# A pad of 32 bytes ahead of the right-hand tiles, and the sums of the down weights moved from the retention stage to the gate/up stage

## The chip, the cores and the metric

The kernel runs on one core of a Trainium2 chip. The metric is device time in microseconds (us). Before the change it is 1449.94 us, the median of 3 runs (1449.83 to 1451.63 us). TensorE is called PE in the rows (its weight loads PEld), VectorE DVE, ScalarE ACT, GpSimd POOL, and SyncE, which issues all DMAs here, SP.

## The reference

One decoder layer for 1024 tokens of 1024 features, in float32:

```python
xn = rmsnorm(h, pre_mix_norm)
mix = token_mixer(xn, ...)            # retention (4 heads) beside latent attention (8 heads), then w_o
h = h + rmsnorm(mix, post_mix_norm)
hn = rmsnorm(h, pre_ffn_norm)
ff = (silu(hn @ w_gate) * (hn @ w_up)) @ w_down      # inner width 2816
h = h + rmsnorm(ff, post_ffn_norm)
e = rmsnorm(p @ w_ple_proj, ple_norm)
h = h + e * sigmoid(h @ w_ple_gate + b_ple_gate)
```

## The kernel before, in words

Every large matmul is done in three products of float32r parts: an operand is split into a high part (a cast on ACT) and a low part (a subtraction, mostly on DVE), and PE adds high by high, high by low and low by high (`split` and `products`, L79 to L95).

The stages follow one another: the input projection, the latent projections, retention (L404 to L547), latent attention (L548 to L675), the output projection with its norms (L686 to L751), gate/up (L756 to L862), down (L864 to L953) and the last gate (`pg`, L955 to L979).

The three matrices of the feed-forward part are multiplied by a Strassen scheme: seven products of half blocks in place of eight, with sums of blocks as operands. The inner width is cut into 11 groups `q`. In gate/up each group has a gate and an up matrix (`m`), each with seven products of 12 matmuls of 128 by 512: 14 steps and 168 matmuls per group, 154 steps and 1848 matmuls in all. Per matrix, SP loads 1 MB (`load`), POOL makes the sums (`weight_sums`, four operations of 128x512), and ACT and DVE split (`weight_part`). Per group POOL makes the sums of the activations (`down_operands`, four operations), which SP stores to `ld`.

Down reads `ld`, `w_down` and `td`: the four sums of blocks of the down weights, t1 = b12 - b11, t2 = b22 - t1, t3 = b22 - b12, t4 = b21 - t2, stored in DRAM. They depend on nothing but the input. Before the change `down_sums(q)` (L408) makes them during retention: two loads of 512 KB into the pool `raws`, four POOL operations of 128x512 (`combos`, L107) into a third `raws` tile and over the loaded ones, three stores (512, 256 and 256 KB). `raws` has four buffers, and the retention weights go through the same four.

The tile framework plans the order of the instructions on each engine when the program is built: work goes ahead of its place in the code where its tiles are free. On the chip each engine and each DMA queue then takes its instructions in that order, and a waiting one holds up those behind it.

Tiles lie in an SBUF partition from the left or from the right (`side="right"`). In the built program the right end is byte 229344, which is 3583 * 64 + 32, and all sizes on that side are multiples of 64, so every right-hand tile starts 32 bytes past a multiple of 64: `bh1` and `bl1` (196576 and 212960), the gate/up weights `graw`, `gh`, `gl` (`gh` from 180192), and the down and last weights `draw`, `dh`, `dl` (`dh` from 135136). The large left-hand tiles start at multiples of 64: `bh0` (19136), `hi` and `lo` of the ring, `xh` and `xl` (19136, 76480), `mh`, `ml`, `h2h`, `h2l`. So the two operands of a matmul are either in step (their distance is a multiple of 64 bytes) or 32 bytes out of step.

In the profile a matmul's names stand as out<-moving,stationary. Of the wide matmuls, these are out of step before the change: all of gate/up (`gu`: moving `xh`, stationary `gh`), all of `pg` (moving `dh_pg`, stationary `h2h`), the output projection `po` at L94 (moving `bh1`), and the second twelve of each 24 in `pqk`, `prg` and `pge` (moving `bh1`, where the first twelve have `bh0`). In step: down (`da`, `db`: both operands on the right) and those first twelve.

Of the kernel before, what the change touches and what calls it, by code (L numbers as in the profile page):

```python
# [11 lines left out]
F32 = mybir.dt.float32  # L12
# [4 lines left out]
ALU = mybir.AluOpType  # L17
# [3 lines left out]
P = 128  # L21
S = 1024
# [11 lines left out]
NQ = NF // 2  # L34
# [28 lines left out]
def hybrid_layer(ctx: ExitStack, tc: tile.TileContext, a: dict, out: bass.AP):  # L63
    nc = tc.nc
    act, dve, pool, pe, sp = nc.scalar, nc.vector, nc.gpsimd, nc.tensor, nc.sync
# [3 lines left out]
    dram = ctx.enter_context(tc.tile_pool(name="dram", bufs=1, space=DRAM))  # L69
# [6 lines left out]
    def ps1(name, tag="t"):  # L76
        return (ps if tag == "t" else psf).tile([P, 512], F32, tag=tag, name=name)
# [29 lines left out]
    def combos(t1, t2, t3, t4, b11, b12, b21, b22, eng):  # L107
        eng.tensor_tensor(out=t1, in0=b12, in1=b11, op=ALU.subtract)
        eng.tensor_tensor(out=t2, in0=b22, in1=t1, op=ALU.subtract)
        eng.tensor_tensor(out=t3, in0=b22, in1=b12, op=ALU.subtract)  # L110
        eng.tensor_tensor(out=t4, in0=b21, in1=t2, op=ALU.subtract)

    def scoped(stack, name, bufs=1, **kw):
        return stack.enter_context(tc.tile_pool(name=name, bufs=bufs, reuse_waits="tile", **kw))
# [6 lines left out]
    def bcast(stack_pool, src, name):  # L121
        t = stack_pool.tile([P, D], F32, name=name, bufs=1)
        sp.dma_start(out=t, in_=src.broadcast_to([P, D]))
        return t

    pack = const.tile([P, sum(PACK.values())], F32, name="pack")
    mhalf = const.tile([P, 32], F32, name="mhalf")
    pool.memset(mhalf, -0.5)
# [16 lines left out]
    od = [dram.tile([P, D], F32, name=f"od{t}") for t in range(NT)]  # L145
    mo = [dram.tile([P, 4, P], F32, name=f"mo{t}") for t in range(NT)]
    ld = [dram.tile([7, P, 512], F32, name=f"ld{q}") for q in range(NQ)]
    td = [dram.tile([4, P, 512], F32, name=f"td{q}") for q in range(NQ)]


    st1 = ExitStack()
# [8 lines left out]
    raws = scoped(st1, "raws", 4)  # L160
# [67 lines left out]
    for t in range(NT):  # L228
# [36 lines left out]
        out=angm,  # L265
        in0=posf.unsqueeze(2).broadcast_to([P, NT, HR]),
        in1=inv.unsqueeze(1).broadcast_to([P, NT, HR]),
        op=ALU.mult,
# [19 lines left out]
    for hf in range(2):  # L288
        for b in (3, 4, 0, 1, 2):
# [3 lines left out]
            w = wq[:, b : b + 1] if b < 3 else wkv[:, b - 3 : b - 2]  # L293
            cs = slice(hf * 512, (hf + 1) * 512)
# [21 lines left out]
    for j in range(NH // 2):  # L316
        pt = ps2(f"pk{j}")
        for hf in range(2):
            cs = slice(hf * 512, (hf + 1) * 512)
# [26 lines left out]
    for j in range(NH // 2):  # L346
        pt = ps2(f"pq{j}")
        for hf in range(2):
            cs = slice(hf * 512, (hf + 1) * 512)
# [45 lines left out]
    for i in range(2):  # L395
        hs, cs = slice(i * RA, (i + 1) * RA), slice(i * H2, (i + 1) * H2)
# [7 lines left out]
    pr = scoped(stk, "pr", 2)  # L404
    tri = pr.tile([P, P], F32, name="tri", bufs=1)
    sp.dma_start(out=tri, in_=a["tri"])

    def down_sums(q):  # L408
        r1, r2, s = [raws.tile([P, S], F32, tag="raw", name=n) for n in ("wd1", "wd2", "wds")]
        sp.dma_start(out=r1, in_=a["w_down"][q][:, 0:2, :].rearrange("p i n -> p (i n)"))  # L410
        sp.dma_start(out=r2, in_=a["w_down"][q][:, 2:4, :].rearrange("p i n -> p (i n)"))
        c0, c1 = slice(0, 512), slice(512, S)
        combos(s[:, c0], s[:, c1], r1[:, c1], r2[:, c0], r1[:, c0], r1[:, c1], r2[:, c0], r2[:, c1], pool)
        sp.dma_start(out=td[q][0:2].rearrange("i p n -> p i n"), in_=s.rearrange("p (i n) -> p i n", i=2))
        sp.dma_start(out=td[q][2], in_=r1[:, c1])
        sp.dma_start(out=td[q][3], in_=r2[:, c0])

    down_q = 0
    g_ret = [1.0 - 2.0 ** (-5.0 - h) for h in range(RH)]
    pending = None  # L420
    for j in range(RH // 2):
# [14 lines left out]
        for hh in range(2):  # L436
            h = 2 * j + hh
# [8 lines left out]
            for hf in range(2):  # L446
                cs = slice(hf * 512, (hf + 1) * 512)
# [28 lines left out]
                for c in range(4):  # L476
                    c1 = slice(c * P, (c + 1) * P)
# [3 lines left out]
                                         in1=tri.unsqueeze(1).broadcast_to([P, 4, P]), op0=ALU.mult, op1=ALU.mult)  # L481
                pkt = ps1("pkt")
                for c in range(4):
                    c1 = slice(c * P, (c + 1) * P)
# [4 lines left out]
                for c in range(4):  # L489
                    c1 = slice(c * P, (c + 1) * P)  # L490
                    pe.matmul(pu[:, c1], kz[:, c1], vt[:, hf * 4 + c, hh * RD : (hh + 1) * RD], start=True, stop=True)
                rs = [rprev]
                for c in range(4):
                    if hf == 1 and c == 3:
                        break
                    c1 = slice(c * P, (c + 1) * P)
# [3 lines left out]
                    else:  # L500
                        dve.scalar_tensor_tensor(out=rn, in0=rs[-1], scalar=_f32(np.exp(np.float32(P) * np.log(np.float32(g_ret[h])))),
                                                 in1=pu[:, c1], op0=ALU.mult, op1=ALU.add)
# [36 lines left out]
                if pending is not None:  # L539
                    pending()  # L540
                pending = finish
                for _ in range(1 + (hf and h > 0)):
                    if down_q < NQ:
                        down_sums(down_q)
                        down_q += 1
        pending()
        pending = None  # L547
    va = pv.tile([P, NT, 2 * VD], F32R, tag="va", name="va")  # L548
# [47 lines left out]
    for h in range(NH):  # L596
        kh_, kl_, qh, ql = heads(h) if h else first
        if h == 2:
            for k in range(RH):
                raw = raws.tile([P, S], F32, tag="raw", name=f"mr{k}")  # L600
                sp.dma_start(out=raw, in_=md[k])
                for c in range(2):
                    cs = slice(c * 512, (c + 1) * 512)
# [8 lines left out]
        for gg in range(2):  # L612
            cs = slice(gg * 512, (gg + 1) * 512)
            po = ps1("po", "of"[gg] if h >= 3 else "o")
            for g in (2 * gg, 2 * gg + 1):
                pb = []
                sc = ps2("sc") if g < 2 else None
                for i in (2 * g, 2 * g + 1):
                    n = (i + 1) * P
                    c1 = slice(i * P, (i + 1) * P)  # L620
# [4 lines left out]
                    w = max(n // nc_, 256)  # L625
                    for c in range(nc_):
                        products(sc[:, o + c * 512 : o + c * 512 + w],
                                 [(qh[:, c1], ql[:, c1], kh_[:, c * w : (c + 1) * w], kl_[:, c * w : (c + 1) * w])])
                    w = n // nc_
# [3 lines left out]
                        out=sv, in0=sv, in1=cmask[:, S - n :].rearrange("p (c n) -> p c n", c=nc_),  # L633
# [122 lines left out]
    st_g = ExitStack()  # L756
# [2 lines left out]
    gs = scoped(st_g, "gs", 3)  # L759
    gev = scoped(st_g, "gev", 1)  # L760
    gga = scoped(st_g, "gga", 2)

    mats = [(name, q) for q in range(NQ) for name in ("w_gate", "w_up")]
    raw, sums, parts, bank, part_sums, act_out = {}, {}, {}, {}, {}, {}
# [26 lines left out]
    def use(m, b, v):  # L791
        name, q = mats[m]
        dst = act_out[q][:, KEPT[b]]
        if name == "w_gate":
            act.activation(dst, v, AF.Silu)
        else:
            dve.tensor_tensor(out=dst, in0=v, in1=dst, op=ALU.mult)  # L797

    def product(m, n):
# [24 lines left out]
        else:  # L824
            nm, blk = {1: ("s1", 0), 4: ("s5", 3), 5: ("u2", 1)}[n]
            dve.tensor_tensor(out=s[nm], in0=dst, in1=s[nm], op=ALU.add)  # L826
            use(m, blk, s[nm])

    def down_operands(q):
        ga = act_out[q]  # L830
        s = gs.tile([P, 3, HALF], F32, tag="s", name="dsums")
        pool.tensor_tensor(out=s[:, 1], in0=ga[:, 2], in1=ga[:, 3], op=ALU.add)  # L832
        pool.tensor_tensor(out=s[:, 0], in0=s[:, 1], in1=ga[:, 0], op=ALU.subtract)
        pool.tensor_tensor(out=s[:, 2], in0=ga[:, 1], in1=s[:, 0], op=ALU.subtract)
        pool.tensor_tensor(out=ga[:, 2], in0=ga[:, 0], in1=ga[:, 2], op=ALU.subtract)
        sp.dma_start(out=ld[q][0:4].rearrange("i p n -> p i n"), in_=ga)
        sp.dma_start(out=ld[q][4:7].rearrange("i p n -> p i n"), in_=s)
# [16 lines left out]
    for i, (m, n) in enumerate(steps):  # L854
        for _, f, args in sorted(todo[i], key=lambda x: x[0]):
            f(*args)
        product(m, n)
        if m % 2 == 0 and m and n == 1:
            down_operands(m // 2 - 1)
    down_operands(NQ - 1)  # L860
    st_g.close()
    st_x.close()  # L862
# [9 lines left out]
    def dslot(srcs, name, sub=dve):  # L872
        n = len(srcs)
        raw = draw.tile([P, D], F32, tag="raw", name=f"raw_{name}")
        for i, src in enumerate(srcs):
            sp.dma_start(out=raw[:, i * (D // n) : (i + 1) * (D // n)] if n > 1 else raw[:, : src.shape[-1]], in_=src)
        m = sum(src.shape[-1] for src in srcs)
        hi, lo = [dring.tile([P, D], F32R, tag=h, name=f"{h}_{name}")[:, :m] for h in ("dh", "dl")]
        split(hi, lo, raw[:, :m], sub=sub)
        return hi, lo  # L880
# [2 lines left out]
        return lambda q: a["w_down"][q][:, i, :]  # L883

    def td_quad(i):
        return lambda q: td[q][i]

    bank_b = [ps1("db", n) for n in "ttfo"]
    bank_a2 = [ps2("da") for _ in range(2)]
    bank_a = [bank_a2[j // 2][:, (j % 2) * HALF : (j % 2 + 1) * HALF] for j in range(4)]  # L890

    def down(li, rhs, banks, fresh):
        for c in range(0, NQ, 2):
            qs = range(c, min(c + 2, NQ))
            lh, ll = dslot([ld[q][li] for q in qs], "l")
            rh, rl = dslot([rhs(q) for q in qs], "r")
            for n, q in enumerate(qs):
                for j in range(4):
                    ls = slice(n * HALF + j * P, n * HALF + (j + 1) * P)
                    rs_ = slice(n * HALF, (n + 1) * HALF)  # L900
                    for m, (l, r) in enumerate(((lh, rh), (lh, rl), (ll, rh))):
                        pe.matmul(banks[j], l[:, ls], r[:, rs_], start=(fresh and q == 0 and m == 0),  # L902
                                  stop=(q == NQ - 1 and m == 2), skip_group_check=True)
# [19 lines left out]
    wpo = bcast(ph, a["w_postf"], "wpo")  # L923
    wpl = bcast(ph, a["w_plen"], "wpl")
    bg = bcast(ph, a["b_pg"], "bg")
    down(4, td_quad(1), bank_b, False)
    for j in range(4):
        act.copy(out=acc[2 * j][:, d2], in_=bank_b[j])
    down(5, td_quad(0), bank_a, True)
    for j in range(4):  # L930
        act.copy(out=acc[2 * j + 1][:, d2], in_=bank_a[j])
    down(6, wd_quad(3), bank_a, False)
    for j in range(4):
        dve.tensor_tensor(out=acc[2 * j][:, d2], in0=bank_a[j], in1=acc[2 * j][:, d2], op=ALU.add)
    down(2, td_quad(2), bank_b, False)
    for j in range(4):
        dve.tensor_tensor(out=acc[2 * j + 1][:, d2], in0=bank_b[j], in1=acc[2 * j + 1][:, d2], op=ALU.add)
    for j in range(4):
# [8 lines left out]

    for j in range(4):
        features(2 * j)
    down(3, td_quad(3), bank_b, False)  # L950
    for j in range(4):
        act.copy(out=acc[2 * j + 1][:, d1], in_=bank_b[j])

# [4 lines left out]
    for n, t in enumerate([0, 2, 4, 6, 1, 3, 5, 7]):  # L958
# [10 lines left out]
        for c in range(2):  # L969
            cs = slice(c * 512, (c + 1) * 512)  # L970
            products(pt[:, cs], [(gh[k // 4][:, k % 4, ts], gl[k // 4][:, k % 4, ts], wg[k][0][:, cs], wg[k][1][:, cs]) for k in range(8)])
        z = draw.tile([P, D], F32, tag="raw", name="z")
        for c in range(2):
            cs = slice(c * 512, (c + 1) * 512)
# [76 lines left out]
```

## Time and profile before

| | |
|---|---|
| median of 3 runs | 1449.94 us |
| the profiled execution | 1453.09 us, of which the span from first to last instruction is 1451.3 us |
| PE busy | 1361.4 us, 94% of the span |
| DVE, ACT, POOL busy | 767.4, 538.5 and 427.2 us |
| mean granted clock of PE | 0.976 of 2.4 GHz |

Busy time of PE counts a matmul from start to modelled end, and matmuls overlap, so how fast they follow one another is read from start to start, or from a run of them in the chain of waits divided by their count.

### The profile page before, as it was taken

To read this page: it belongs to the slowest core of one execution; us is meant where nothing else is said; L and a number is where in the kernel's file an instruction comes from. 1 tells how busy PE (TensorE), PEld (TensorE's weight loads), DVE (VectorE), ACT (ScalarE), POOL (GpSimd) and SP (SyncE) were. 2 spreads that over 40 slices of the span, in tenths; PEclk is the share of its full clock that TensorE was granted. 3 is DMA by queue.
4 is the path that set the end of the run, shared out by engine and by line. 5 is a ranking of instruction groups with operands and counts; after the bars stand their busy time and mean duration, and the time that the engine had idled before them with its cause. 6 is when DMAs were issued, how large, how long until landed. Compare 5 with 4: busy or idle time off the path is not lost.

```text
span 1451.3 us, 18194 instructions
## 1 busy us (share of the span) xinstructions
PE 1361.4 (94%) x6732; PEld 1134.0 (78%) x6732; DVE 767.4 (53%) x1198; ACT 538.5 (37%) x889; POOL 427.2 (29%) x333
## 2 busy tenths in 40 slices
PE   7999999999989998876899999999997999999998
PEld 6987988788768886655688888888885788888776
DVE  6456447526577675586344444434443554474653
ACT  5343221111565554344233333333332544444421
POOL 1100344400354243237144444444443000013300
PEclk9999999999999999986999999999999999999999
DMA  6137776812565641661123332232312966575422
GB/s 242 44 123 247 264 266 232 284 52 59 163 202 145 177 113 45 226 236 50 38 109 110 109 109 92 98 109 87 109 58 98 330 203 204 187 239 181 132 72 73
DMA packets 91320, 214.73 MB, mean 148 GB/s; under 512 B 9504, under 2 KB 24096, under 8 KB 88416
## 3 DMA queue, kind: packets, MB, share of 16 engines
q1 hardware_dynamic: 91232, 213.58, 44.2%
q8 instruction: 53, 0.87, 0.3%
q14 instruction: 35, 0.29, 0.1%
HBM read 144.86 MB, written 67.63 MB: 146 GB/s over the span
## 4 chain that ended last, share of the span: by engine, by line
PE 70%; DMA 8%; DVE 7%; issue 5%; POOL 5%; ACT 3%; SPq 1%; DVEq 0%; POOLq 0%; ACTq 0%
PE gu L813 30%; PE da L902 6%; PE pg L94 5%; PE fill L94 4%; PE pa L94 4%; PE db L902 3%; PE sc L94 3%; DMA wd<-in_w_down 2%; PE prg L94 2%; PE ptp L650 2%; PE prv L94 2%; PE pge L94 2%; PE pqk L94 1%; PE po L94 1%; DMA td<-wd 1%
## 5 line engine op out<-in xcount | busy, mean ns | idle before, releaser
L813 PE MATMUL gu<-xh,gh_w_gate 128*128 128x512 f32 x308 | 123.0, 399 | 5.1 <-ACT gh_w_gate L81 1.6
L813 PE MATMUL gu<-xh,gh_w_up 128*128 128x512 f32 x308 | 122.4, 398 | 2.3 <-DVE s L826 0.9
L813 PE MATMUL gu<-xh,gl_w_up 128*128 128x512 f32 x308 | 121.9, 396 | 1.6 <-DVE gl_w_up L82 1.6
L813 PE MATMUL gu<-xl,gh_w_gate 128*128 128x512 f32 x308 | 122.5, 398 | 0.0
L813 PE MATMUL gu<-xh,gl_w_gate 128*128 128x512 f32 x308 | 122.3, 397 | 0.0
L813 PE MATMUL gu<-xl,gh_w_up 128*128 128x512 f32 x308 | 122.0, 396 | 0.0
L119 POOL TENSOR_TENSOR s<-s,mhalf 128x1 f32<-128x1 f32 x32 | 28.6, 901 | 310.3 <-DVE s L117 310.2
L641 POOL TENSOR_TENSOR pr<-pr,ri 128x128 f32<-128x128 f32 (+3 forms) x64 | 73.8, 1164 | 109.3 <-DVE ri L640 97.3
L82 DVE TENSOR_TENSOR dl_r<-raw_r,dh_r 128x1024 fp32r<-128x1024 f32 (+1 forms) x42 | 47.7, 1135 | 81.9 <-ACT dh_r L81 70.4
L832 POOL TENSOR_TENSOR dsums<-ga 128x512 f32<-128x512 f32 x11 | 14.2, 1289 | 250.4 <-DVE ga L797 250.4
L826 DVE TENSOR_TENSOR s<-gu,s 128x512 f32<-128x512 f32 x44 | 30.4, 691 | 102.0 <-PE gu L813 102.0
L81 ACT CAST dh_r<-raw_r 128x1024 fp32r<-128x1024 f32 (+1 forms) x42 | 41.3, 982 | 105.9 <-PE da L902 52.4
L902 PE MATMUL db<-dh_r,dh_l 128*128 128x512 f32 x176 | 68.1, 397 | 8.3 <-ACT dh_r L81 8.3
L813 PEld LDWEIGHTS gu<-xh,gh_w_gate 128*128 128x128 f32 x308 | 58.3, 189 | 20.6 <-ACT gh_w_gate L81 2.0
L813 PEld LDWEIGHTS gu<-xh,gh_w_up 128*128 128x128 f32 x308 | 57.9, 188 | 17.8 <-DVE s L826 1.3
L813 PEld LDWEIGHTS gu<-xh,gl_w_up 128*128 128x128 f32 x308 | 57.9, 188 | 16.0 <-DVE gl_w_up L82 2.1
L902 PE MATMUL db<-dl_r,dh_l 128*128 128x512 f32 x176 | 69.3, 394 | 0.1
L813 PEld LDWEIGHTS gu<-xh,gl_w_gate 128*128 128x128 f32 x308 | 58.2, 189 | 14.3 <-DVE gl_w_gate L82 0.2
L902 PE MATMUL db<-dh_r,dl_l 128*128 128x512 f32 x176 | 69.3, 394 | 0.0
L813 PEld LDWEIGHTS gu<-xl,gh_w_gate 128*128 128x128 f32 x308 | 58.3, 189 | 14.0
L813 PEld LDWEIGHTS gu<-xl,gh_w_up 128*128 128x128 f32 x308 | 58.0, 188 | 13.9
L82 DVE TENSOR_TENSOR tl<-ptp,th 128x512 fp32r<-128x512 f32 (+1 forms) x80 | 49.7, 633 | 24.0 <-ACT th L81 22.8
(337 smaller groups left out, 3807.2 us busy)
## 6 DMA issues: line engine op xcount, KB each, us to landing
raw_l<-ld SPq DMA_DIRECT2D x77, 256.0 KB, 3.3
wd<-in_w_down SPq DMA_DIRECT2D x22, 512.0 KB, 4.7
raw_w_gate<-in_w_gate SPq DMA_DIRECT2D x11, 1024.0 KB, 4.8
raw_w_up<-in_w_up SPq DMA_DIRECT2D x11, 1024.0 KB, 4.8
ld<-ga SPq DMA_DIRECT2D x11, 1024.0 KB, 4.3
raw_r<-td SPq DMA_DIRECT2D x44, 256.0 KB, 4.0
ld<-dsums SPq DMA_DIRECT2D x11, 768.0 KB, 3.6
raw_r<-in_w_down SPq DMA_DIRECT2D x33, 256.0 KB, 4.6
```

The lines of the kernel that those rows point to most:

```text
L81: act.copy(out=hi, in_=src)
L82: sub.tensor_tensor(out=lo, in0=src, in1=hi.bitcast(F32), op=ALU.subtract)
L94: pe.matmul(dst, l, r, start=(m == 0), stop=(m == n - 1))
L119: pool.tensor_tensor(out=dst, in0=dst, in1=mhalf[:, :n], op=ALU.pow)
L641: pool.tensor_tensor(out=pr_[:, :n], in0=pr_[:, :n], in1=ri.broadcast_to([P, n]), op=ALU.mult)
L650: pe.transpose(pt[:, m * P : (m + 1) * P], pb[qq][:, kk * P : (kk + 1) * P], ident)
L813: pe.matmul(dst, l[:, at, ks], r[:, i, k, :], start=(n in (0, 1, 3) and x == 0), stop=(x == 11), skip_group_check=True)
L826: dve.tensor_tensor(out=s[nm], in0=dst, in1=s[nm], op=ALU.add)
L832: pool.tensor_tensor(out=s[:, 1], in0=ga[:, 2], in1=ga[:, 3], op=ALU.add)
L902: pe.matmul(banks[j], l[:, ls], r[:, rs_], start=(fresh and q == 0 and m == 0), stop=(q == NQ - 1 and m == 2), skip_group_check=True)
```

## The change

A pool `pad` with one tile of 8 floats (32 bytes) is opened first on the right, so each right-hand tile starts 32 bytes lower: `bh1` at 196544, `gh` from 180160, `dh` from 135104. Nothing reads or writes the tile.

`down_sums` leaves retention. In gate/up, after steps 2, 5, 8 and 11 of the 14 of each group, `down_sums(q, c)` treats a quarter of the columns: one load of 256 KB (four pieces of 512 bytes per partition) into a tile of the new left-hand pool `gd` with one buffer, four POOL operations of 128x128 that write over the loaded blocks, one store of 256 KB. That is 44 loads, 176 POOL operations and 44 stores. `td` is laid out as [P, 4, 512] instead of [4, P, 512], its blocks in the order T1, T3, T4, T2, and down picks them by these names. The same sums are computed.

```diff
+    pad = ctx.enter_context(tc.tile_pool(name="pad", bufs=1, side="right"))
+    pad.tile([P, 8], F32, name="pad")
...
-    td = [dram.tile([4, P, 512], F32, name=f"td{q}") for q in range(NQ)]
+    td = [dram.tile([P, 4, 512], F32, name=f"td{q}") for q in range(NQ)]
...
-    def down_sums(q):
-        r1, r2, s = [raws.tile([P, S], F32, tag="raw", name=n) for n in ("wd1", "wd2", "wds")]
-        sp.dma_start(out=r1, in_=a["w_down"][q][:, 0:2, :].rearrange("p i n -> p (i n)"))
-        sp.dma_start(out=r2, in_=a["w_down"][q][:, 2:4, :].rearrange("p i n -> p (i n)"))
-        c0, c1 = slice(0, 512), slice(512, S)
-        combos(s[:, c0], s[:, c1], r1[:, c1], r2[:, c0], r1[:, c0], r1[:, c1], r2[:, c0], r2[:, c1], pool)
-        sp.dma_start(out=td[q][0:2].rearrange("i p n -> p i n"), in_=s.rearrange("p (i n) -> p i n", i=2))
-        sp.dma_start(out=td[q][2], in_=r1[:, c1])
-        sp.dma_start(out=td[q][3], in_=r2[:, c0])
...
-                for _ in range(1 + (hf and h > 0)):
-                    if down_q < NQ:
-                        down_sums(down_q)
-                        down_q += 1
...
+    gd = scoped(st_g, "gd", 1)
+
+    def down_part():
+        return gd.tile([P, 4, P], F32, name="wd")
...
+    T1_, T3_, T4_, T2_ = range(4)
+
+    def down_sums(q, c):
+        w = down_part()
+        cs = slice(c * P, (c + 1) * P)
+        b11, b12, b21, b22 = [w[:, i] for i in range(4)]
+        sp.dma_start(out=w, in_=a["w_down"][q][:, :, cs])
+        pool.tensor_tensor(out=b11, in0=b12, in1=b11, op=ALU.subtract)
+        pool.tensor_tensor(out=b12, in0=b22, in1=b12, op=ALU.subtract)
+        pool.tensor_tensor(out=b22, in0=b22, in1=b11, op=ALU.subtract)
+        pool.tensor_tensor(out=b21, in0=b21, in1=b22, op=ALU.subtract)
+        sp.dma_start(out=td[q][:, :, cs], in_=w)
...
+        if i % 14 % 3 == 2:
+            down_sums(i // 14, i % 14 // 3)
...
-        return lambda q: td[q][i]
+        return lambda q: td[q][:, i, :]
```

## Rows read from the trace of the kernel before

**Rows 1.** Stages: us, then busy us (xcount) of PE, PEld, DVE, ACT, POOL; PEclk, DMA share, GB/s.

```profile
210.00:290.00 80.00, 74.56 (x421) 63.63 (x420) 55.60 (x107) 12.27 (x15) 37.49 (x31) 0.98 0.76 258
290.00:358.00 68.00, 68.00 (x405) 59.50 (x404) 29.67 (x63) 10.08 (x17) 2.01 (x2) 1.00 0.18 50
676.00:1115.00 439.00, 431.89 (x1835) 345.62 (x1836) 185.74 (x196) 146.19 (x199) 186.90 (x126) 0.99 0.26 93
```

**Rows 2.** Chain of waits, gate/up: start us, us, what.

```profile
709.97 397.88 PE gu L813 x1704
```

**Rows 3.** Chain of waits, down.

```profile
1160.51 29.92 PE da L902 x132
```

**Rows 4.** Timeline of PE, one product of 24: its matmuls 2 and 13, and the next product.

```profile
97.44 0.39 PE L94 MATMUL pge<-bl,hi_r 128*128 128x512 f32 x1
...
99.94 0.40 PE L94 MATMUL pge<-bh,hi_r 128*128 128x512 f32 x1
...
102.75 0.40 PE L94 MATMUL pk<-hi_ct,hi_kv 128*128 128x512 f32 x1
```

**Rows 5.** Groups by line and shape, PE: one group of gu, pqk, pg and po.

```profile
L813 PE MATMUL gu<-xh,gh_w_gate 128*128 128x512 f32 x308 | 123.0, 399 | 5.1 <-ACT gh_w_gate L81 1.6 <-ACT s L821 1.4 <-DVE s L826 1.2
...
L94 PE MATMUL pqk<-bh,hi_r 128*128 128x512 f32 x128 | 51.7, 404 | 0.0
...
L94 PE MATMUL pg<-dh_pg,h2l 128*128 128x512 f32 x128 | 51.2, 400 | 0.0
...
L94 PE MATMUL po<-bh,ml 128*128 128x512 f32 x64 | 26.5, 415 | 0.0
```

**Rows 6.** Waits of PE, retention (160 to 360 us): us, times, longest.

```profile
PE pgt L535 <- DVE gn L530: 3.0, 2, 2.0
```

**Rows 7.** Chain of waits, retention: a load of down weights, then the norm's POOL step.

```profile
220.51 4.67 DMA wd<-in_w_down
...
226.58 0.10 POOL gf L119
```

**Rows 8.** Waits, gate/up: POOL's, and those of the DMA queue (SPq).

```profile
POOL dsums L832 <- DVE ga L797: 250.4, 11, 31.8
...
SPq L769 <- DVE gl_w_gate L82: 183.3, 10, 23.4
```

**Rows 9.** Timelines of POOL, ACT, DVE and PE, gate/up: from a sum to its product.

```profile
814.69 1.29 POOL L775 TENSOR_TENSOR sums<-sums,raw_w_up 128x512 f32<-128x512 f32 x1
...
816.01 1.05 ACT L81 CAST gh_w_up<-sums 128x1024 fp32r<-128x1024 f32 x1 [1.55 <-POOL sums L775]
...
817.09 1.23 DVE L82 TENSOR_TENSOR gl_w_up<-sums,gh_w_up 128x1024 fp32r<-128x1024 f32 x1 [3.51 <-ACT gh_w_up L81]
...
824.87 0.40 PE L813 MATMUL gu<-xh,gh_w_up 128*128 128x512 f32 x1
```

**Rows 10.** Groups by line and shape, POOL: 128x128, and 128x512 twice.

```profile
L641 POOL TENSOR_TENSOR pr<-pr,ri 128x128 f32<-128x128 f32 x8 | 3.2, 404 | 10.1 <-DVE ri L640 10.1
...
L834 POOL TENSOR_TENSOR dsums<-ga,dsums 128x512 f32<-128x512 f32 x11 | 25.1, 2278 | 0.0
...
L832 POOL TENSOR_TENSOR dsums<-ga 128x512 f32<-128x512 f32 x11 | 14.2, 1289 | 250.4 <-DVE ga L797 250.4
```

**Rows 11.** DMA issues: xcount, KB each, median us from issue to landing.

```profile
raw_l<-ld SPq DMA_DIRECT2D x77, 256.0 KB, 3.3
wd<-in_w_down SPq DMA_DIRECT2D x22, 512.0 KB, 4.7
...
td<-wd SPq DMA_DIRECT2D x22, 256.0 KB, 2.2
```

**Rows 12.** Groups by shape, DVE in gate/up: two subtractions of one shape.

```profile
L82 DVE TENSOR_TENSOR gl_w_up<-raw_w_up,gh_w_up 128x1024 fp32r<-128x1024 f32 x22 | 42.2, 1917 | 7.9 <-ACT gh_w_up L81 7.9
...
L82 DVE TENSOR_TENSOR gl_w_gate<-raw_w_gate,gh_w_gate 128x1024 fp32r<-128x1024 f32 x22 | 28.5, 1294 | 43.3 <-ACT gh_w_gate L81 42.4
```

**Rows 13.** Waits of the whole run: PE ahead of gate/up.

```profile
PE ptx L699 <- DVE mix L728: 12.0, 3, 5.6
```

More of the change, by code (lines that the diff above doesn't have):

```diff
@@ L406, in hybrid_layer @@
     sp.dma_start(out=tri, in_=a["tri"])
-    def down_sums(q):
-        r1, r2, s = [raws.tile([P, S], F32, tag="raw", name=n) for n in ("wd1", "wd2", "wds")]
-        sp.dma_start(out=r1, in_=a["w_down"][q][:, 0:2, :].rearrange("p i n -> p (i n)"))
-        sp.dma_start(out=r2, in_=a["w_down"][q][:, 2:4, :].rearrange("p i n -> p (i n)"))
-        c0, c1 = slice(0, 512), slice(512, S)
-        combos(s[:, c0], s[:, c1], r1[:, c1], r2[:, c0], r1[:, c0], r1[:, c1], r2[:, c0], r2[:, c1], pool)
-        sp.dma_start(out=td[q][0:2].rearrange("i p n -> p i n"), in_=s.rearrange("p (i n) -> p i n", i=2))
-        sp.dma_start(out=td[q][2], in_=r1[:, c1])
-        sp.dma_start(out=td[q][3], in_=r2[:, c0])
-    down_q = 0
     g_ret = [1.0 - 2.0 ** (-5.0 - h) for h in range(RH)]
@@ L925, in hybrid_layer @@
     bg = bcast(ph, a["b_pg"], "bg")
-    down(4, td_quad(1), bank_b, False)
+    down(4, td_quad(T2_), bank_b, False)
     for j in range(4):
         act.copy(out=acc[2 * j][:, d2], in_=bank_b[j])
-    down(5, td_quad(0), bank_a, True)
+    down(5, td_quad(T1_), bank_a, True)
     for j in range(4):
@@ L934, in hybrid_layer @@
         dve.tensor_tensor(out=acc[2 * j][:, d2], in0=bank_a[j], in1=acc[2 * j][:, d2], op=ALU.add)
-    down(2, td_quad(2), bank_b, False)
+    down(2, td_quad(T3_), bank_b, False)
     for j in range(4):
@@ L949, in hybrid_layer @@
         features(2 * j)
-    down(3, td_quad(3), bank_b, False)
+    down(3, td_quad(T4_), bank_b, False)
     for j in range(4):
```

## The prediction

> **What bounds the kernel now.** I read the stages first [rows 1]: in gate/up PE is busy 431.9 of 439 us, from 290 to 358 us 68.00 of 68, in the busy part of retention 74.56 of 80. So time comes off where PE does less or goes faster, and other engines' time counts only where PE waits for them. Then how fast PE goes, from the chain of waits, where a run of matmuls without a wait stands as one piece. In gate/up 1704 matmuls of 512 columns take 397.88 us, 233.5 ns each [rows 2]; in down 132 of the same shape take 29.92 us, 226.7 ns each [rows 3]. The granted clock is the same in both, near 1.00. What differs? In gate/up the moving and the stationary operand are 32 bytes out of step, in down in step. One product has both cases with the rest equal: in `pge` the first twelve matmuls move `bh0`, in step with the weights, the second twelve `bh1`, out of step. From matmul 2 to matmul 13 are 11 steps in 2.50 us, 227.3 ns each; from matmul 13 to the next product 12 steps in 2.81 us, 234.2 ns each [rows 4]. The weights' tiles, the stage and the engines around are the same. So a 512-column matmul out of step costs 6.8 to 6.9 ns more here, and down, where both tiles are off a multiple of 64, shows that the distance counts and not either place.
>
> **The pad.** It moves all right-hand tiles by 32 bytes, which puts every product that is out of step into step and leaves down in step (both its operands move). The work is the same; the term is count times 6.8 ns (233.5 less 226.7).
> - Gate/up: six groups of 308 [rows 5] are 1848 matmuls: 12.6 us.
> - `pg`: three groups of 128 [rows 5], 384: 2.6 us.
> - `pqk`: half of three groups of 128 [rows 5], 192: 1.3 us. `prg` and `pge` each have two heads, two halves and 24 matmuls, half of them out of step: 48 and 48, 0.65 us.
> - `po`: three groups of 64 [rows 5], 192: 1.3 us if PE bounds it. Its stage has waits of PE up to 5.6 us [rows 13], so I take half, 0.65 us, between 0 and 1.3.
>
> Sum 17.8 us, 18.4 at most. What stands behind it: in gate/up PE's faster pace must not run into the next limit. A group shrinks from 168 * 233.5 ns = 39.2 us to 38.1 us. The sums of an up matrix end at 815.98, its split at 818.32, and its product begins at 824.87 [rows 9]: 6.5 us of room, of which the faster pace takes about 0.3.
>
> The trace doesn't show the new distance: every pair in step in these rows is apart by a multiple of 512 bytes, and after the pad the moved pairs are apart by 256 past one (`gh` - `xh` = 161024 = 314 * 512 + 256). That is the unknown of this term; its other end is 0 and has a rival below.
>
> One rule speaks against the whole term. The Trainium skill (TensorE: Matmul & The Clock Gate, "Step-by-step: what each phase is for") says that PE has one read port for the moving operand and another for the weights, so that loading the next weights takes nothing from the running matmul. By that rule the distance of the two tiles couldn't matter and the pad would give 0. The `pge` rows don't agree with it, 227.3 against 234.2 ns in one product [rows 4], so I go by the rows.
>
> **Retention without the sums.** This takes 22 loads, 33 stores and 44 POOL operations away, and three of the turns of `raws` per group. PE's loss there is the stage's idle time, 80 - 74.56 = 5.4 us, and its half-speed clock, 2% of 80 us, 1.6 us [rows 1]; 3.0 us of the idle time are two waits of `pgt` for the normalised head [rows 6]. That normalisation takes one POOL step, which stood in POOL's order behind a sum whose load was issued at 220.51 and took 4.67 us; the step ran at 226.58 [rows 7]. Without the sums nothing is ahead of it. In the later part, with the sums done, PE doesn't idle at all (68.00 of 68) [rows 1]. Gain 7.0 us at most and 0 at least; I take 6, near the later part's row.
>
> **The sums in gate/up.** 176 POOL operations of 128x128 at 0.404 us [rows 10] are 71 us, 6.5 us per group. POOL waits there 250.4 us in 11 waits for the activations [rows 8], 22.8 us per group, so they fit, and PE waits for none of them. Upper price: POOL and DVE slow each other when both work from SBUF (POOL's 128x512 takes 1289 or 2278 ns [rows 10], DVE's subtraction 1294 or 1917 [rows 12]), so 1.77 times as much, 2.9 us for the four. The Trainium skill (SBUF — State Buffer, "Who interferes with whom") has this as a lock: a DVE instruction with two SBUF inputs and a POOL instruction that reads SBUF block one another for a whole instruction. The rows agree in kind, and change no term.
>
> The added waits: the four operations wait for their load, and POOL's next work (`dsums`, `sums`) queues behind; the store waits for POOL on SP, and the loads of weights and the stores of `ld` queue behind it. A late load therefore costs 3.3 us, as 256 KB take in down, to 4.7, as 512 KB [rows 11], and with the operations at most 4.7 + 2.9 = 7.6 us, against 6.5 of room [rows 9]: 1.1 us a group, 12 us in all, if it happens in every group, and 0 if the planner puts the operations into POOL's wait. I take 2, near 0, since SP too stands idle there, 183.3 us in ten waits for the gate buffers alone [rows 8]. Down reads `td` in the same pieces of 2 KB: 0. That the order of everything is planned anew I leave at 0 with one wait like the longest ahead of gate/up, 5.6 us, either way [rows 13].
>
> **The sum.** -17.8 - 6 + 2 = -21.8 us. The profiled execution, 1453.09 us (span 1451.3 and 1.8 around it), would come to 1431.3; it is 3.15 us above the median of the runs, 1449.94, so the forecast for the median is 1428.1, say 1428.
>
> **Rivals.**
> 1. *The pace stays* (the distance of 256 past a multiple of 512 is no better than 32 past one of 64, or the unused pad tile takes no room): the 17.8 fall away, 1449.94 - 6 + 2 = 1446. For it: the unseen distance, and the skill's rule of two ports, which gives this same time. Against: the rows show that 32 bytes matter, and none speaks for a period as coarse as 512.
> 2. *The queue falls behind* (slower than before). One `wd` tile makes load, four operations and store one chain. By the rows it takes 3.3 + 1.6 + 2.2 = 7.1 us [rows 10, 11]; with 4.7 us each for load and store and 2.9 for POOL 12.3. A group of 38.1 us holds four: from 9.5 us per part on, SP no longer keeps up, and the raw weights behind the parts come late. In that case PE goes at SP's pace: at 10.5 us, 44 parts cost 44 us less the 6.5 of room, so 1428 + 37 = 1465. For it: in retention these sums did sit on the chain, and POOL came late to the norm [rows 7]. If the planner runs parts ahead more tightly than the chip, it starts below 9.5 us. Against: DMA share is 0.26 in gate/up, 0.76 in retention [rows 1], and loads of 256 KB at 3.3 us are from a stage that is busier than gate/up.
> 3. *Retention keeps its waits* under another name: 1434.
>
> **How the numbers follow.** Forecast with rival 3 as its edge: 74%. Rival 1: 13%. Rival 2: 13%, of which 9 above 1453 and 4 short of it. A difference of 0.2% (2.9 us) is about what a measurement of this kernel can tell. Faster by more: 72 + 7 + 3 = 82%; within: 2 + 5 + 2 = 9%; slower: 9%. The range goes from 1428 less the 9 that the bounds leave (0.6 of `po`, 1 of retention, 2 of the moved sums, 5.6 of the new order), 1419, up to rival 1 at 1446; what it leaves out is rival 2 and little else.
>
> **What would show it.** Right: one run of `gu` in the chain at about 227 ns per matmul and gate/up near 420 us; `pg` at the pace of down; no wait of `pgt` for `gn`, and PE idle under 1 us from 210 to 290; POOL in gate/up busier by some 70 us with PE's idle time unchanged. Wrong: `gu` still at 233.5 ns (rival 1); PE waits in gate/up for `gh` or `gl` behind `sums` or raw loads, with SP waiting for `wd` (rival 2); waits ahead of gate/up that grow by more than 5.6 us.

## The result, and the profile after

The changed kernel took 1502.08 us (median of 4 runs, 1498.97 to 1505.99) against 1449.88 before: a ratio of 1.0366, 95% interval 1.0332 to 1.0401. That is 74 us above the forecast of 1428 and far outside the range. Of the rivals, 2 comes nearest: the chain of the one `wd` tile fell behind, at twice the price, 74 us over the forecast where it was given 37. But not by the path that it names: the raw weights weren't late (POOL waited 3.2 us for them in all of gate/up), POOL's own sums were.

The stages in the changed kernel (us, then busy us and count of PE, PEld, DVE, ACT, POOL; PEclk, DMA share, GB/s), to be held against [rows 1]:

```profile
210.00:290.00 80.00, 80.00 (x515) 72.47 (x514) 43.18 (x102) 9.66 (x17) 4.03 (x4) 1.00 0.19 57
290.00:358.00 68.00, 67.55 (x371) 58.27 (x370) 37.70 (x95) 9.26 (x13) 3.02 (x3) 1.00 0.17 47
676.00:1115.00 439.00, 386.77 (x1608) 314.09 (x1607) 161.39 (x171) 127.20 (x175) 239.13 (x264) 0.94 0.39 130
```

Retention did what was hoped: PE no longer idles from 210 to 290, and with the pad's part in it gate/up began at 661.86 us instead of 676.51 (671.26 with the pad alone). The loss is all in gate/up, which lasted 506.5 us instead of 442.8. From 676 to 1115 us PE did 1608 matmuls instead of 1835, at a mean granted clock of 0.94. What was waited for in gate/up (662 to 1168 us: us in total, times, longest):

```profile
POOL wd L827 <- DMA wd<-in_w_down: 208.2, 32, 8.8
...
ACT gh_w_up L81 <- POOL sums L765: 86.0, 10, 10.0
...
PE gu L803 <- ACT s L811: 55.8, 12, 6.8
```

This is a chain from a load to PE. Ten of the twelve waits of PE are 4.9 to 6.8 us long, one per group. One of them, followed through the engines (timelines of POOL, ACT and PE: start us, us, what, idle before and its releaser):

```profile
857.17 0.46 POOL L827 TENSOR_TENSOR wd<-wd 128x128 f32<-128x128 f32 x1 [5.81 <-DMA wd<-in_w_down]
...
858.66 1.29 POOL L836 TENSOR_TENSOR dsums<-ga 128x512 f32<-128x512 f32 x1
...
865.27 1.26 POOL L765 TENSOR_TENSOR sums<-sums,raw_w_up 128x512 f32<-128x512 f32 x1
...
877.89 0.79 POOL L830 TENSOR_TENSOR wd<-wd 128x128 f32<-128x128 f32 x1
```

```profile
866.57 1.05 ACT L81 CAST gh_w_up<-sums 128x1024 fp32r<-128x1024 f32 x1 [8.11 <-POOL sums L765]
867.52 0.58 ACT L811 COPY s<-gu 128x512 f32<-128x512 f32 x1
```

```profile
862.89 0.39 PE L803 MATMUL gu<-xh,gl_w_gate 128*128 128x512 f32 x1
868.15 0.80 PE L803 MATMUL gu<-xh,gh_w_up 128*128 128x512 f32 x1 [4.88 <-ACT s L811]
```

POOL stood at the load of a part, and behind that part were the sums of the group. They run in one batch with `dsums`, from 858.66. The cast on ACT waited 8.11 us for `sums`, and the copy of a finished PSUM result stood behind the cast in ACT's order. PE's next product needed that copy and waited 4.88 us. The ten waits come 45.2 to 46.2 us apart, where a group was expected to take 38.1.

The load was late because one `wd` tile makes load, operations and store a chain. SP's issues around it (start us, us, what):

```profile
842.90 0.53 SPq L831 DMA_DIRECT2D td<-wd  x1
845.48 0.57 SPq L826 DMA_DIRECT2D wd<-in_w_down  x1
851.38 0.53 SPq L831 DMA_DIRECT2D td<-wd  x1
853.96 0.57 SPq L826 DMA_DIRECT2D wd<-in_w_down  x1
854.63 0.57 SPq L759 DMA_DIRECT2D raw_w_gate<-in_w_gate  x1
861.65 0.53 SPq L831 DMA_DIRECT2D td<-wd  x1
```

Store to load is 2.58 us, store to store 8.5 and 10.3 us. From one batch to the next POOL's order has four parts, one of them with its operations spread through the batch. So the group is the batch, 858.66 to 878.68, 20.0 us, and then three parts at about 8.5 us: 45.5 us. That is the distance of PE's waits; that this loop sets PE's pace is what the experiments test.

The wait costs a second time. Three stretches around it (columns as above): the wait, what followed, the rest of the group:

```profile
862.00:868.15 6.15, 1.28 (x6) 0.74 (x4) 0.50 (x1) 1.53 (x2) 6.15 (x6) 1.00 0.54 176
868.15:871.50 3.35, 3.35 (x8) 2.67 (x9) 1.32 (x2) 0.63 (x1) 3.35 (x3) 0.50 0.54 208
871.50:905.00 33.50, 33.50 (x149) 27.73 (x148) 15.28 (x16) 11.08 (x15) 13.42 (x19) 1.00 0.39 128
```

After the idle time the granted clock was 0.50 (1.2 of 2.4 GHz) for 3.35 us. In all of gate/up 116 matmuls began more than 330 ns before the next one, which didn't wait; they took 24.2 us more than 226.7 ns each would; in the kernel below without the sums there were 17, with 3.0 us. So of the 77.0 us by which gate/up is longer than there (506.5 less 429.5), 53.7 are waits and 21.2 half clock; what the other 2 are stays open.

### The profile page after: what moved, and what is told of

It is laid out like the page before. It is cut to its first block, busy times and chain, and to the rows that moved or that the text cites. A ratio compares the mean times of both kernels' runs of the same rounds, so it can differ in the third digit from the quotient of the medians.

```text
span 1499.4 us, 18388 instructions
## 1 busy us (share of the span) xinstructions
PE 1364.2 (91%) x6732; PEld 1146.6 (76%) x6732; DVE 758.4 (51%) x1198; ACT 538.6 (36%) x889; POOL 458.4 (31%) x465
## 4 chain that ended last, share of the span: by engine, by line
PE 49%; POOL 19%; DMA 17%; issue 7%; DVE 5%; ACT 3%; SPq 1%; POOLq 0%; DVEq 0%; ACTq 0%
DMA td<-wd 7%; DMA wd<-in_w_down 6%; PE db L908 6%; PE pqk L94 6%; PE da L908 6%; PE pg L94 5%; PE pa L94 4%; PE prv L94 3%; PE fill L94 3%; PE sc L94 3%; POOL sums L765 2%; POOL sums L767 2%; POOL wd L828 2%; POOL wd L827 1%; PE prg L94 1%
## 5 line engine op out<-in xcount | busy, mean ns | idle before, releaser
L803 PE MATMUL gu<-xh,gh_w_up 128*128 128x512 f32 x308 | 130.3, 423 | 56.0 <-ACT s L811 54.4
L803 PE MATMUL gu<-xh,gl_w_up 128*128 128x512 f32 x308 | 127.1, 413 | 0.6 <-DVE gl_w_up L82 0.6
L803 PE MATMUL gu<-xl,gh_w_up 128*128 128x512 f32 x308 | 127.5, 414 | 0.0
L803 PEld LDWEIGHTS gu<-xh,gh_w_up 128*128 128x128 f32 x308 | 62.7, 204 | 75.0 <-ACT s L811 59.0
L119 POOL TENSOR_TENSOR gf<-gf,mhalf 128x4 f32<-128x4 f32 x8 | 8.1, 1007 | 266.7 <-DVE gf L117 266.7
L827 POOL TENSOR_TENSOR wd<-wd 128x128 f32<-128x128 f32 x44 | 23.1, 525 | 208.2 <-DMA wd<-in_w_down 208.2
L82 DVE TENSOR_TENSOR gl_w_up<-sums,gh_w_up 128x1024 fp32r<-128x1024 f32 (+1 forms) x22 | 25.1, 1140 | 109.0 <-ACT gh_w_up L81 109.0
L803 PEld LDWEIGHTS gu<-xh,gl_w_up 128*128 128x128 f32 x308 | 62.2, 202 | 15.0 <-DVE gl_w_up L82 1.1
L803 PEld LDWEIGHTS gu<-xl,gh_w_up 128*128 128x128 f32 x308 | 62.9, 204 | 13.1
```

The source lines that it names most:

```text
L82: sub.tensor_tensor(out=lo, in0=src, in1=hi.bitcast(F32), op=ALU.subtract)
L119: pool.tensor_tensor(out=dst, in0=dst, in1=mhalf[:, :n], op=ALU.pow)
L803: pe.matmul(dst, l[:, at, ks], r[:, i, k, :], start=(n in (0, 1, 3) and x == 0), stop=(x == 11), skip_group_check=True)
L827: pool.tensor_tensor(out=b11, in0=b12, in1=b11, op=ALU.subtract)
```

## The experiments

Theory A: the order of instructions was planned tighter than the chained loads, operations and stores run on the chip, and the queue that stands at a part (POOL's or SP's) holds up the weight sums. Theory B: the added work itself, wherever it stands, is too much for POOL, SP or the DMA engines.

**The two parts of the change, each alone.**

```diff
# e1_pad_only: the kernel before, and
+    pad = ctx.enter_context(tc.tile_pool(name="pad", bufs=1, side="right"))
+    pad.tile([P, 8], F32, name="pad")
# e1b_pad64: the kernel before, the same pool, and
+    pad.tile([P, 16], F32, name="pad")
# e2_move_only: the changed kernel without the two lines of the pad
```

> The kernel before with the pad alone; the sums of the down weights stay in retention. If the pad's term was sized rightly: 17.8 us off, 1432 us, and gate/up runs at 227 ns per matmul without a wait. If the pad has a part in the slowdown (tiles on the right moved, another plan): over 1450 us.

> The kernel before with a pad of 64 bytes in place of none: all right-hand tiles start 64 bytes lower and stay 32 bytes past a multiple of 64. If the distance of the two operands of a matmul, modulo 64, sets the pace: gate/up stays at 233.5 ns per matmul, and the time at that of the kernel before, within 3 us. If the pad brings its gain in some other way (any shift of the tiles, or the order planned anew): near the 1434 us of the pad of 32 bytes.

> The changed kernel without the pad, so only the move of the sums. Theory A (gate/up goes at the pace of a loop of load, POOL, store and POOL's other sums, 45.5 us a group, and PE waits for what is left): PE's slower pace of 39.2 us a group still lies inside the loop, so gate/up stays at about 506 us, and only the 5 us of pad outside it are lost: 1507 us. If PE's waits come on top of PE's own time whatever its pace: 17.8 us more, 1520 us.

The pad alone: 1434.02 us, ratio 0.9906 (0.9878 to 0.9934). The pad of 64 bytes, which keeps the operands 32 bytes out of step: 1448.22 us, ratio 0.9998 (0.9979 to 1.0017). The long run of `gu` in the chain of waits (start us, us, what), first with 32 bytes, then with 64:

```profile
704.51 386.58 PE gu L815 x1704
```

```profile
701.71 397.88 PE gu L815 x1704
```

226.9 and 233.5 ns per matmul; the second is to the hundredth what [rows 2] shows. So neither the shift nor a new order makes the gain: the distance of the operands does, and 256 bytes past a multiple of 512 is as good as 0. Other multiples of 64 weren't run, so that each of them will do is not shown. The move alone: 1507.92 us, where theory A had 1507, ratio 1.0415 (1.0393 to 1.0438), with ten waits of PE for the copy, 3.3 to 6.3 us each. With the move the pad is worth 6 us and not 15: where the loop of parts sets the pace, faster matmuls for the most part wait longer. All of PE's idle time in gate/up is 61.4 us with the pad and 55.0 without, and gate/up takes 506.5 and 511.4 us.

**Gate/up without the sums, and without POOL's share of them.**

```diff
# e3_no_sums: the changed kernel, and
-        if i % 14 % 3 == 2:
-            down_sums(i // 14, i % 14 // 3)
...
-        return lambda q: td[q][:, i, :]
+        return lambda q: a["w_down"][q][:, i, :]
# e4_no_pool: the changed kernel without the four tensor_tensor of down_sums
```

> The changed kernel with the sums in neither place: they are left out, and down reads blocks of the down weights where it would read the sums (same transfers). It shows what pad and an undisturbed retention give together. From the profile of the changed kernel, gate/up began 14.7 us earlier; with 16.5 us of pad from there on: 1449.9 - 14.7 - 15.9 = 1419 us. By the prediction's terms (17.8 and 6): 1426 us.

> The changed kernel with the four POOL operations of a part left out: load and store of each part stay in gate/up, on the same queue. Theory A (POOL's weight sums queue behind operations that wait for a load): the waits of PE are gone, 1419 to 1424 us. Theory B (SP's queue holds up the raw weights, or the DMA traffic does): the waits stay, 1470 us or more.

Without the sums, down reading blocks of `w_down` in their place: 1424.45 us, between the 1419 and the 1426 of the expectation, ratio 0.9849 (0.9819 to 0.988). Gate/up takes 429.5 us, and PE doesn't wait at all between its first 40 us and its last 25 (chain of waits):

```profile
695.62 386.58 PE gu L803 x1704
```

Without POOL's operations but with the loads and stores: 1466.65 us, ratio 1.0129 (1.0103 to 1.0155), between the two theories. Its waits in gate/up:

```profile
POOL sums L764 <- DMA raw_w_gate<-in_w_gate: 44.2, 5, 10.8
...
PE gu L803 <- ACT s L811: 34.1, 7, 8.4
```

Here POOL waits five times for the 1 MB load of `w_gate`. SP has stores and loads of parts ahead of it, each issued some 2.6 to 3 us behind the one before, about the time that one takes to land (start us, us, what):

```profile
856.93 0.53 SPq L827 DMA_DIRECT2D td<-wd  x1
859.51 0.57 SPq L826 DMA_DIRECT2D wd<-in_w_down  x1
860.18 0.67 SPq L759 DMA_DIRECT2D raw_w_gate<-in_w_gate  x1
```

The order takes more parts per group now. The last part's store goes out at 926.31 us, and after the fifth of PE's long waits, at 917 us, there are no more. So the chain holds up SP's queue just as it does POOL's: taking work from one engine moved the stall to the other.

**The order on ACT.** Is the cast ahead of the copy the cause, or only where it shows?

```diff
# e8_cast_after_copy: the changed kernel, and
-            when(i - 3, 2, weight_part, m, p)
+            when(at_step[m, 0] + 1 if p == 1 and m >= 2 else i - 3, 2, weight_part, m, p)
...
-        split(hi, lo, src)
+        if p == 1 and (m, 0) in copied:
+            with tc.issue_after(copied[m, 0].ins):
+                split(hi, lo, src)
+        else:
+            split(hi, lo, src)
```

> The changed kernel with the order on ACT altered: the cast of the up sums stands behind the copy that frees PE's bank, not ahead of it. Theory A (the loop of four chained parts and the batch of sums takes 43 to 45 us per group, and the copy is only where it shows): PE no longer waits for the copy but for gh_w_up or gl_w_up, or again for another eviction, and the group stays at 43 us or more, 1475 to 1502 us. Theory C (the cast ahead of the copy is the cause, since it takes away the room of 6.5 us up to the product): the waits vanish, 1428 to 1445 us.

1484.68 us, ratio 1.0254 (1.0237 to 1.0271). PE's waits from 720 to 1140 us:

```profile
PE gu L808 <- DVE s L821: 41.1, 10, 5.8
```

The wait went to the next queue: DVE's addition `s` now stands behind the subtraction for `gl_w_up`, which needs the same cast. That is worth 17 us, but the waits still come 43 to 46 us apart. Theory C of that run, by which the cast's place is the whole cause, falls; A holds.

**How many parts stand between two batches.**

```diff
# e6_three_parts: the changed kernel, down reads w_down as in e3, and
-        if i % 14 % 3 == 2:
+        if i % 14 in (2, 5, 8):
# e6h_three_held: the same three, at steps 10, 11 and 12, the operations under
+        with tc.issue_after(batch_end[0]):     # the group's last weight sum
```

> The changed kernel with three of the four parts per group; down reads blocks of w_down in place of td, so the stored sums are not used and a quarter of them isn't made. POOL's order in this kernel still takes four parts between two batches of weight sums, as in the changed kernel, until its 33 parts are used up, after about 8 groups. Theory A: PE waits in those 8 groups and not in the last two: 1424 + 8 * 7.7 = 1486 us (1470 to 1490). Theory B (each part costs its share wherever it stands): waits in all groups, three quarters as long, 1424 + 0.75 * 77 = 1482 us. The time is nearly the same; the place of the waits tells them apart.

> As the kernel with three of four parts, but the POOL operations of a group's three parts are held behind the last weight sum of that group, so that exactly three parts stand between two batches of sums. The same 33 loads, 132 operations and 33 stores; down reads blocks of w_down in place of td, and a quarter of the sums isn't made. Theory A: the batch takes 17.5 us; three parts with one buffer take 2.2 + 2 * (2.6 + 3.1 + 2.2) = 18 us, together 35.5 us of a group of 38.1, so nearly no wait: 1424 to 1436 us. Theory B (the work itself): as without the hold, 1475 to 1490 us.

Three parts: 1477.85 us, ratio 1.0205 (1.0183 to 1.0228). Seven waits of PE for the copy from 720 to 1010 us, none from 1010 to 1120:

```profile
PE gu L803 <- ACT s L811: 33.6, 7, 5.1
```

So it isn't the number of parts in the whole stage that counts (theory B wanted shorter waits in every group) but how many the order puts between two batches. With exactly three, the same work took 1449.49 us (ratio 1.0019, 0.9991 to 1.0046): 28 us less, but 13 above the bound that A gave. Its ten runs spread from 1443 to 1460 us, and the trace is of one at 1455.64. Its waits from 720 to 1080 us show why:

```profile
POOL sums L765 <- DMA raw_w_gate<-in_w_gate: 34.8, 8, 6.6
...
PE gu L804 <- ACT s L812: 16.5, 8, 4.3
```

The operations fit, but SP's order has the 1 MB load of `w_gate` behind the last part's store and the load after it (issued at 835.97, 838.55 and 839.22; the sum that needs it began at 845.85). My sum for this run counted POOL and not what SP has queued.

**Two buffers, without and with the hold.**

```diff
# e5_two_buffers: the changed kernel, parts of 104 columns (the last 96), five per group,
# after steps 2, 4, 7, 9 and 12
-        return gd.tile([P, 4, P], F32, name="wd")
+        return gd.tile([P, 4, 104], F32, name="wd", bufs=2)
# e5h_two_held: the same after steps 9 to 13, the four operations under
+        with tc.issue_after(batch_end[0]):
# e5h_no_pad: e5h without the two lines of the pad
```

> The changed kernel with two wd buffers instead of one: five parts per group (four of 104 columns, one of 96) instead of four of 128, the same sums, the same pad. Theory A (the chain load, four operations, store of the one buffer runs longer on the chip than the order on POOL allows for, so POOL stands at a part's load with the weight sums behind it): with a second buffer the next load doesn't wait for the store, the waits of PE for the copy s vanish in nearly all groups, gate/up takes about 430 us, 1424 to 1440 us in all. Theory B (the added work itself, 220 operations on POOL and the loads and stores on SP and the DMA engines, delays the weight sums whatever the buffers): the ten waits of 5 to 7 us stay, 1480 us or more.

> The changed kernel with two wd buffers and five parts per group (104 columns, the last 96), and the POOL operations of a group's parts held behind its last weight sum, so that exactly five parts stand between two batches. All sums are made. Theory A (the order is planned tighter than the chained loads and stores run, and POOL's and SP's queues hold up the weight sums): five parts in pairs take about 17 us after a batch of 17.5 us, 34.5 of a group of 38.1 us, and the 1 MB load of w_gate, which stands behind the last store on SP, has some 2 to 3 us to spare: waits of PE for the copy under 1.5 us each, 1425 to 1440 us. Theory B (the added work itself): 1450 us or more, as without the hold.

> The kernel with two buffers and the parts held behind the batch, without the pad: the move of the sums alone, in an order that leaves the weight sums in time. The prediction's terms: 1449.9 - 6 (retention) + 2 (sums in gate/up) = 1446 us. By the later runs (retention gave 9.6 us, the sums cost 3 us): 1427.7 + 15.4 = 1443 us, and gate/up at 441 to 442 us, 233.5 ns per matmul. If the faster pace of the pad was needed for the order to work, or the slower pace gives the batch still more room, it shows as waits of PE for the copy, or as none. A time near 1500 us would say that it was the pad, not the hold, that let the sums through.

Two buffers alone: 1452.98 us, ratio 1.0036 (1.0018 to 1.0054), 49 us better than the changed kernel but 13 worse than I had given theory A. POOL's operations still stand between the sums as the plan packed them:

```profile
POOL wd L828 <- DMA wd<-in_w_down: 77.1, 36, 4.8
...
PE gu L803 <- ACT s L811: 17.5, 7, 3.6
```

With the hold as well: **1427.69 us, ratio 0.9862 (0.9843 to 0.9881)**, faster than both kernels, and every sum is made. The run of `gu` in its chain, and two of POOL's rows at the end of a group:

```profile
698.32 387.46 PE gu L804 x1704
```

```profile
868.31 0.91 POOL L833 TENSOR_TENSOR wd<-wd 128x96 f32<-128x96 f32 x1
869.85 1.29 POOL L839 TENSOR_TENSOR dsums<-ga 128x512 f32<-128x512 f32 x1 [0.63 <-DVE ga L788]
```

In this group POOL is through with the parts before the activations are there, and the batch waits for DVE, as it did in the kernel before [rows 8]. The margin is small: six such waits from 720 to 1080 us, 0.6 us at most, where they were up to 31.8 us before. POOL still waits for part loads, but PE doesn't wait at all in these 360 us. Gate/up takes 430.3 us, 0.8 more than without the sums, though this kernel makes 220 operations and 55 loads and stores where the changed one makes 176 and 44. That rules theory B out. Without the pad the same kernel takes 1439.74 us, ratio 0.993 (0.9905 to 0.9955), gate/up 441.4 us: the move in this order is worth 10 us by itself, and the pad 12 on top. That is 3 us below the 1443 of the expectation and 6 below the 1446 by the prediction's terms.

**Another place for the sums.**

```diff
# e7_in_attention: the changed kernel without gd; in latent attention, four buffers
+        w = pm.tile([P, 4, P], F32, name="wd", bufs=4)
...
+        with tc.issue_after(behind.ins):
...
+                    if turn < 4 * NQ:
+                        down_load(turn)
+                    if 2 <= turn < 4 * NQ + 2:
+                        down_sums(turn - 2, scaled)    # scaled: POOL's scaling of pr_
```

> The pad and the sums in place, but the 44 parts stand in the latent attention stage, with four buffers, and the POOL operations of a part are held behind POOL's scaling of the row tile two after the one at which its load stands. All sums are made; gate/up has none. The changed kernel without the sums took 1424.5 us: if the sums cost nothing here, 1424 to 1428 us. If POOL's scaling of the probabilities comes late behind the parts (71 us of operations in about 290 us of the stage, and loads that may land late), PE waits for the transposed probabilities and it is 1430 to 1445 us.

1456.49 us, ratio 1.0059 (1.0041 to 1.0077): worse than either expectation. Gate/up is as good as without the sums (429.5 us), but it begins at 694.97 us instead of 664.10. The same stretch of attention with the sums in it, and in the kernel without sums:

```profile
358.00:500.00 142.00, 121.73 (x686) 105.95 (x686) 85.72 (x193) 75.87 (x162) 101.86 (x162) 0.93 0.83 246
```

```profile
358.00:500.00 142.00, 133.82 (x790) 117.45 (x789) 95.19 (x225) 87.82 (x186) 63.57 (x55) 0.96 0.58 174
```

DMA is 0.83 busy and PE loses 12 us. PE's waits from 358 to 690 us grew for `ptp <- POOL pr` (9.6 us, where 1.0), for `po <- ACT th` (8.2, where 1.0), for `fill <- DVE lo_o` (6.2, where none) and for `sc <- ACT pr` (5.1, where 1.2). Which share of the 31 us is POOL's order and which late loads wasn't separated.

## Why the prediction was wrong, point by point

**The pad: right.** Predicted -17.8 us, of which 12.6 in gate/up. Measured alone -15.4; in gate/up 1704 matmuls take 11.30 us less, at that pace 12.25 for all 1848. In `pg` 144 matmuls take 32.94 us against 33.85 out of step, 6.3 ns each (chains of waits, the kernel before and then the pad alone):

```profile
1410.37 33.85 PE pg L94 x144
```

```profile
1393.64 32.94 PE pg L94 x144
```

Rival 1 is out. The Trainium skill (TensorE: Matmul & The Clock Gate, "Step-by-step: what each phase is for") gives PE two independent read ports, one for the moving operand and one for the weights. The prediction drew from it that the distance has no effect; 226.9 against 233.5 ns doesn't agree with that. Two slips in the working moved nothing: rival 2 has a chance of 4% of ending short of 1453 us, but the sums of the chances count 3 and 2 for it; and the sign "gate/up near 420 us" left out the waits and the half clock at the stage's two ends; with the pad alone it took 431.2.

**Retention: right in kind, too small.** Predicted -6, at most 7; the pad with undisturbed retention gives 9.6 us more than the pad alone (1434.02 less 1424.45). Attention began 10.8 us earlier (its first score at 346.9 instead of 357.8), the pad alone bringing 0.8; at the start of gate/up 7.2 us are left of the other 10 (671.26 with the pad alone, 664.10 without the sums). The bound counted PE's idle time and half clock, 7.0 us. From the first `prv` to the first score the stage takes 195.2 us with the pad alone and 186.1 without the sums, 9.1 less; so some 2 us more lay in matmuls, mostly of `pqk` and `pgt`, which followed one another more closely afterwards without the trace showing a wait before. What had held them stays open.

**The sums in gate/up: the step that failed.** Predicted +2, at most 12; measured +77.6 (1502.08 less 1424.45). Three readings in it were wrong.
- *The room.* I measured it from the split of `sums` to the product that uses it, 6.5 us [rows 9]. But the cast on ACT that waits for the sums has a copy behind it that PE needs sooner. In the kernel before, the cast already waited 1.55 us [rows 9]. ACT's copy behind it, and the product of PE that comes next for the same matrix, from the timelines of before:

```profile
816.96 0.58 ACT L821 COPY s<-gu 128x512 f32<-128x512 f32 x1
```

```profile
819.27 0.40 PE L813 MATMUL gu<-xh,gh_w_up 128*128 128x512 f32 x1
```

The copy ends at 817.54, the product starts at 819.27: 1.7 us were left, not 6.5. The prediction did ask who is queued behind a waiting instruction, but for POOL and SP alone.
- *The point from which rival 2 decides.* I divided the group by four, 9.5 us per part. But POOL is taken by the batch of sums for 17.5 us of each group, 807.44 to 824.92 in the kernel before (its first and last row on POOL's timeline):

```profile
807.44 1.29 POOL L832 TENSOR_TENSOR dsums<-ga 128x512 f32<-128x512 f32 x1 [21.73 <-DVE ga L797]
...
823.17 1.75 POOL L777 TENSOR_TENSOR sums<-raw_w_gate,sums 128x512 f32<-128x512 f32 x1
```

The parts must go through beside it, in the rest: 38.1 - 17.5 = 20.6 us for three, 6.9 us each. The 7.1 us that I had worked out from the rows was already above that. The chip took 8 to 10: the operations 0.53 to 0.64 us on the mean, not 0.40, the loads 3.1 us and the stores 2.6 (DMA issues of the changed kernel: count, KB, median us to landing):

```profile
wd<-in_w_down SPq DMA_DIRECT2D x44, 256.0 KB, 3.1
td<-wd SPq DMA_DIRECT2D x44, 256.0 KB, 2.6
```

- *What a late part costs.* A wait of 5 us is not only 5 us: some 2 us of half clock come after it.

The forecast of 1428 came within 1 us of a kernel with two buffers and the hold. That is no credit to it: the price of 2 us, "if the planner puts the operations into POOL's wait", took for granted an order that the changed kernel doesn't have.

## What to carry to other kernels

Room is measured on every in-order queue that the late thing passes, up to the first instruction behind it that the bounding engine needs; a product's own operand may have 6 us while a copy behind its cast has 1.7. A chain through one buffer has to fit into what the engine's other work leaves of the period, not into the period, and an order planned ahead may pack it tighter than the chip runs it: two buffers and an explicit hold behind the urgent work took 77 us of loss to 3. And an edit that makes the bounding engine faster shows its worth only where nothing else has become the bound, here 6 us in place of 12 to 15.

## What the runs showed of the hardware that was not expected

- The pace of a 128x512 float32r matmul depends on the distance of its two operands in the partition: 226.7 ns at a multiple of 512 bytes [rows 3], 226.9 at 256 past one, and 233.5 at 32 past a multiple of 64, before the change and after the right-hand operand had moved by 64. Other distances weren't measured.
- Around the ten long waits of PE in the changed kernel, 4.9 to 6.8 us of idle time, its granted clock fell to 0.50 each time; after the wait of 4.9 us at 863 it stayed there for 3.35 us.
- POOL's 128x128 operations over one tile took 0.46 us at best in gate/up and 0.53 to 0.64 us on the mean, where another operation of that shape, in attention of the kernel before, took 0.40 [rows 10]. Whether the operation, the shared buffer or DVE's work beside it makes the difference, no run took apart.
